# Conditioning weights as the stationary operand in the first modulation of a hybrid diffusion block

## The chip, the core and the metric

One core of a Trainium2 chip runs one program. The metric is the device time of one execution in microseconds (us), and less is better.

## The reference, cut to what matters

The block takes 512 latent tokens and 256 context tokens of width 1024, a conditioning vector `c` and a learned vector `c_ctx`. Everything starts with a modulation: the first 2048 columns of `w_mod` give a shift and a scale for each of the 1024 features, once for the latents and once for the context.

```python
silu_c = jax.nn.silu(c)
silu_cc = jax.nn.silu(c_ctx)
sh_a, sc_a, g_a, sh_f, sc_f, g_f = [m[:, None, :] for m in jnp.split(silu_c @ w_mod[l] + b_mod[l], 6, axis=-1)]
mod_c = jnp.split(silu_cc @ w_mod[l][:, :n_mod * D_MODEL] + b_mod[l][:n_mod * D_MODEL], n_mod, axis=-1)
hc = ctx * (1.0 + mod_c[1]) + mod_c[0]
hx = x * (1.0 + sc_a) + sh_a
```

`hx` and `hc` then go through one input projection `w_in` (z, q, the scan inputs, dt, keys, values), a state-space scan, attention, an output projection and a mixture of experts. All is float32.

## The kernel before, in words

The kernel holds activations turned: `xT` and then `hxh`/`hxl` are [feature in partition, 8 k-tiles, 768 tokens], tokens 0 to 255 context and 256 to 767 latents. Most products are made of three passes over a split of each operand into a high and a low float32r part (`mm3`, L111); the modulation uses plain float32 (`mm`, L108).

`sil` (L215) is [128, 8 k-tiles, 32]: columns 0 and 1 of each k-tile are silu of `c` and `c_ctx`, the other thirty are zero (L216).

The modulation is done in four quarters, h = 0 to 3. `quarter_spec` (L180) says what a piece of weights is: for k-tile kt and quarter h, 256 columns of shift and 256 of scale, [128, 2, 256], 256 KB. A `Stream` (L30) loads pieces over SP's DMA queue (L53) into twelve buffers "mraw" (L198 to L200) and gives them out in order with `take`. A quarter serves the two feature tiles 2h and 2h + 1.

`mod_quarter` (L242) makes one quarter. For each k-tile, a group of four multiplications has 32 columns of `sil` as the stationary operand and 128 columns of weights moving; the four write the four strips of 32 partitions of one PSUM tile "m" (one buffer), [128, 128], in which rows 0 and 1 of a strip are the two conditions. After eight k-tiles VectorE copies "m" to `msb` (L250), PE turns it through the identity into another PSUM tile (L252), and VectorE adds the bias twice (L256) and 1 to the scales (L258), into `modT`: [feature, condition, 16], shift and scale by feature.

`hx_tile` (L261) applies them to one feature tile: two tensor-scalar operations on VectorE (L263), the high part on ScalarE (L265), the low part on VectorE (L266). `x_turn` (L233) turns the token tiles `xin` into `xT`: for each feature tile six PE transposes through PSUM tiles "b" or "t" and copies on ScalarE (L239) and VectorE (L240).

`kv_pass` (L285) is the first user of hx: for each k-tile 6 token tiles x 3 passes = 18 multiplications, 288 moving columns (dt and keys).

Order of work: input loads, `x_turn` of tiles 0 and 1, quarter 0, `x_turn` of 2 and 3, hx tiles 0 and 1, `kv_pass` of k-tiles 0 and 1; then quarters 1, 2, 3 with their hx tiles, the rest of `x_turn` after quarter 1 and `kv_pass` of k-tile 2; k-tile 3 is queued behind the last group of quarter 3 (L309). A planner of the framework turns this program into one queue per engine. It goes by priority (program order, changed by `rank`, L117) and by its own idea of when operands are there; quarters 1 to 3 have a rank ahead of `kv_pass` (L301). So groups of the modulation, turns and key/value multiplications stand mixed in PE's queue, which runs in that order. SP's queue also runs in order: a load whose buffer isn't free holds back the loads behind it, the second half of the input (`x_load(256, 768)`, L273) among them.

The other modulation vectors (gates and the second shift and scale) come later from `mod_rest` (L690) with another function; it uses a PSUM tile "m" and buffers "wraw" of its own.

Of the kernel before, what the change touches and what calls it, by code (L numbers as in the profile page):

```python
# [8 lines left out]
F32 = mybir.dt.float32  # L9
# [86 lines left out]
def hybrid_block_kernel(ctx: ExitStack, tc: tile.TileContext, I, out):  # L96
    nc = tc.nc
    PE, V, S, G, SP = nc.tensor, nc.vector, nc.scalar, nc.gpsimd, nc.sync

    def pool(name, bufs=1, side="left", space=None, stack=None):  # L100
        kw = dict(name=name, bufs=bufs, reuse_waits="tile")
        if space is not None:
            kw["space"] = space
        else:
            kw["side"] = side
        return (stack or ctx).enter_context(tc.tile_pool(**kw))

    def mm(o, a, b, first, last):  # L108
        return PE.matmul(o, lhsT=a, rhs=b, start=first, stop=last)  # L109
# [34 lines left out]
    psa = [pool("psa", 3, space=PSUM, stack=psa_st)]  # L144
# [4 lines left out]
    def pb(tag="b", dt=F32):  # L149
        return psb.tile([128, 512], dt, name=tag, bufs=tags.get(tag, 1))  # L150
# [8 lines left out]
    ident, tri_le, tri_ge = cst[:, 0:128], cst[:, 128:256], cst[:, 256:384]  # L159
# [8 lines left out]
    xtp = pool("xtp", stack=xst)  # L168
# [46 lines left out]
    sil = const.tile([128, 8, 32], F32, name="sil")  # L215
# [25 lines left out]

    def mod_quarter(h):  # L242

        ps = psa[0].tile([128, 512], F32, name="m", bufs=1)[:, 0:128]
        for kt in range(8):
            w = mod0[h].take()
            for i in range(4):
                last = mm(ps[32 * i:32 * i + 32, :], sil[:, kt, :], w[:, i // 2, i % 2 * 128:i % 2 * 128 + 128], kt == 0, kt == 7)
        msb = xtp.tile([128, 128], F32, name="msb", bufs=2)
        V.tensor_copy(msb, ps)  # L250
        p = pb("s" if h == 0 else "t")[:, 0:128]
        PE.transpose(p, msb, ident)  # L252
        pv = p.rearrange("p (s f z) -> p z s f", s=2, f=2)
        part = lambda a: a.rearrange("p (s f) -> p s f", s=2)[:, :, 2 * h:2 * h + 2]
        for r in range(2):
            V.tensor_add(part(modT[:, r, :]), pv[:, r], part(cols[:, C_BM:C_BM + 16]))  # L256
        o = slice(8 + 2 * h, 10 + 2 * h)
        V.tensor_scalar_add(modT[:, :, o], modT[:, :, o], 1.0)  # L258
        return last
# [7 lines left out]

    x_turn(range(2))
    mod_quarter(0)
    win.deep = win.ahead = 0  # L270
    win.fill(0)
# [22 lines left out]
    def six():  # L294
        return dict(zip(order, [pa() for _ in range(3)] + [pb(), pb(), pb("s")]))

    kv_start = tc.cur_priority
    ps = six()
    kv_pass(ps, range(2), 288, 2)
    for h in (1, 2, 3):  # L300
        with rank(kv_start - 3000 + 1000 * h):  # L301
            last = mod_quarter(h)
            if h == 1:
                x_turn(range(4, 8))
        for kt in (2 * h, 2 * h + 1):
            hx_tile(kt)
        if h == 1:
            kv_pass(ps, range(2, 3), 288, 2)
# [54 lines left out]
    ps = six()  # L363
# [440 lines left out]
    def part(g, t, y):  # L804

        p = pa() if g else pb("t")
        for k in range(4):
            PE.transpose(p[:, k * 128:(k + 1) * 128], y[:, k * 128:(k + 1) * 128], ident)
        m = parts[g, t] = (mix, mix2)[g].tile([128, 2, 4, 128], F32R, name=("wraw", "a")[g], bufs=4)
        pv = p.rearrange("p (k q) -> p k q", k=4)  # L810
        S.activation(m[:, 0], pv, AF.Copy)
        V.tensor_sub(m[:, 1], pv, f32(m[:, 0]))
# [843 lines left out]
```

## Time and profile before

| what | us |
|---|---|
| median of 3 runs | 896.88 |
| lowest and highest of them | 889.95, 919.74 |
| the profiled execution | 891.73 |
| its span from the first to the last instruction | 889.9 |

Times in the rows are from the start of the span. Engines: PE is TensorE's multiplications, PEld its loads of the stationary operand, DVE is VectorE, ACT ScalarE, POOL GpSimd, SPq the SyncE queue that issues DMAs. A float32 multiplication leaves two records of MATMUL and two of LDWEIGHTS. The duration of a record includes its way through the engine, so records that follow each other overlap: n like records in T with one lasting d follow at (T - d) / (n - 1). PEclk is the clock granted to TensorE as a share of 2.4 GHz.

### The profile page before, as it was taken

The page shows a single profiled execution, that of the slowest core. Times are in us where ns is not written, and L with a number is a line of the kernel's source. Part 1 is how long each engine was busy: PE and PEld are TensorE (multiplying, and loading weights), DVE is VectorE, ACT ScalarE, POOL GpSimd, SP SyncE. Part 2 cuts the span into 40 slices and gives each one's busy share as a digit, 9 for nine tenths or more (in the row PEclk, how much of TensorE's full clock was granted, in tenths as well). Part 3 has the DMA queues.
Part 4 walks back from the last instruction along what each step waited for, and adds up shares of the span by engine and source line. Part 5 has one row for each costly group of instructions (what it writes and reads, how often), then busy time and mean ns, then how long its engine had stood idle before and what let it go on. Part 6 is the DMA issues. An engine that isn't in the chain of part 4 may idle for free.

```text
span 889.9 us, 14409 instructions
## 1 busy us (share of the span) xinstructions
PE 798.8 (90%) x5328; PEld 604.5 (68%) x5328; DVE 630.3 (71%) x1042; ACT 455.0 (51%) x870; POOL 268.0 (30%) x202
## 2 busy tenths in 40 slices
PE   6998999898989989899999899999982999999783
PEld 3696676566777568677777777787862777777562
DVE  3576665786857896573646566666987999889677
ACT  2253442656743353364544645656461766777452
POOL 0012212313321052510159344600011355544421
PEclk8999999999999999999999999999995999999997
DMA  9966987446522144566052111300459999999964
GB/s 308 321 193 230 299 292 251 124 125 199 144 73 80 30 130 131 194 197 207 18 194 73 36 35 42 119 13 1 143 195 324 343 342 341 338 325 344 341 181 167
DMA packets 112369, 165.59 MB, mean 186 GB/s; under 512 B 13032, under 2 KB 78088, under 8 KB 112296
## 3 DMA queue, kind: packets, MB, share of 16 engines
q1 hardware_dynamic: 105720, 141.76, 49.2%
q0 software_dynamic: 6288, 21.84, 8.6%
q8 instruction: 42, 0.69, 0.3%
q10 hardware_dynamic: 288, 1.05, 0.3%
q14 instruction: 31, 0.25, 0.1%
HBM read 142.41 MB, written 22.21 MB: 185 GB/s over the span
## 4 chain that ended last, share of the span: by engine, by line
PE 59%; DMA 14%; DVE 11%; ACT 6%; issue 5%; POOL 3%; SPq 1%; DVEq 0%; POOLq 0%; ACTq 0%
PE a L109 24%; PE s L109 13%; PE t L109 7%; PE b L963 3%; DMA wraw<-in_w_mod_dram 3%; PE v L109 3%; PE b L109 3%; DMA bc<-csd 2%; PE m L109 2%; DVE acc L475 2%; ACT hxh L957 1%; PE b L1368 1%; DMA wraw<-in_w_up_dram 1%; DMA ml<-in_w_down_dram 1%; DMA ml<-in_w_up_dram 1%
## 5 line engine op out<-in xcount | busy, mean ns | idle before, releaser
L76 ACT ACTIVATE whi<-wraw 128x1024 fp32r<-128x1024 f32 (+1 forms) x100 | 104.2, 1045 | 62.7 <-PE a L109 31.9
L78 DVE TENSOR_TENSOR wlo<-wraw,whi 128x1024 fp32r<-128x1024 f32 (+1 forms) x75 | 95.7, 1282 | 29.3 <-ACT whi L76 29.3
L78 POOL TENSOR_TENSOR wlo<-wraw,whi 128x1024 fp32r<-128x1024 f32 (+1 forms) x20 | 49.3, 2464 | 150.6 <-ACT whi L76 132.2
L956 DVE TENSOR_REDUCE mx<-s 128x1 f32<-128x768 f32 x64 | 61.1, 955 | 29.6 <-PE s L109 24.4
L957 ACT ACTIVATE hxh<-s,mx 128x768 f32<-128x768 f32 x64 | 57.5, 898 | 41.1 <-DVE mx L956 39.5
L475 DVE SCALAR_TENSOR_TENSOR acc<-u,cols,acc 128x770 f32<-128x770 f32 (+1 forms) x48 | 55.4, 1153 | 30.3 <-ACT acc L467 24.3
L109 PE MATMUL a<-whi,hxh 128*128 128x512 f32 (+2 forms) x176 | 69.1, 394 | 1.5 <-ACT hxh L265 1.5
L109 PE MATMUL a<-wlo,hxh 128*128 128x512 f32 (+2 forms) x176 | 69.1, 393 | 0.2 <-DVE wlo L78 0.2
L109 PE MATMUL a<-whi,hxl 128*128 128x512 f32 (+2 forms) x176 | 67.9, 387 | 0.0
L109 PE MATMUL a<-hxh,whi 128*128 128x512 f32 (+1 forms) x176 | 62.5, 355 | 0.0
L109 PE MATMUL a<-hxl,whi 128*128 128x512 f32 (+1 forms) x176 | 62.2, 354 | 0.0
L109 PE MATMUL a<-hxh,wlo 128*128 128x512 f32 (+1 forms) x176 | 61.7, 350 | 0.0
L963 PE MATMUL b<-cst,hxh 128*128 128x128 f32 x384 | 58.7, 277 | 1.7 <-DVE hxh L967 0.5
L592 ACT ACTIVATE bc<-bc,lb 128x128 f32<-128x128 f32 x128 | 40.5, 390 | 23.6 <-POOL bc L589 20.4
L963 PEld LDWEIGHTS b<-cst,hxh 128*128 128x128 f32 x384 | 43.5, 141 | 11.4 <-ACT hxl L937 4.0
L967 DVE COPY hxh<-b 128x512 f32<-128x512 f32 x48 | 33.0, 687 | 16.9 <-PE b L963 16.7
L109 PE MATMUL a<-whi,xh 128*128 128x512 f32 x102 | 44.4, 436 | 0.0
L589 POOL TENSOR_SCALAR_AFFINE_SELECT bc<-bc 128x512 f32<-128x512 f32 x32 | 26.5, 835 | 52.4 <-DMA bc<-csd 50.4
L109 PE MATMUL a<-whi,xl 128*128 128x512 f32 x102 | 41.3, 405 | 0.0
L109 PE MATMUL a<-wlo,xh 128*128 128x512 f32 x102 | 41.2, 404 | 0.0
L1417 POOL DMA_INDIRECT acc<-y,rowi x15 | 28.2, 1881 | 40.8 <-DVE wlo L78 19.4
L109 PEld LDWEIGHTS a<-wlo,hxh 128*128 128x128 f32 x176 | 33.8, 192 | 9.9 <-issue 5.3
(467 smaller groups left out, 2123.2 us busy)
## 6 DMA issues: line engine op xcount, KB each, us to landing
wraw<-in_w_mod_dram SPq DMA_DIRECT2D x32, 512.0 KB
wraw<-in_w_in_dram SPq DMA_DIRECT2D x30, 512.0 KB
wraw<-in_w_down_dram SPq DMA_DIRECT2D x22, 512.0 KB
wraw<-in_w_gate_dram SPq DMA_DIRECT2D x40, 256.0 KB
wraw<-in_w_up_dram SPq DMA_DIRECT2D x40, 256.0 KB
mraw<-in_w_mod_dram SPq DMA_DIRECT2D x32, 256.0 KB
bc<-csd SPq DMA_DIRECT2D x32, 256.0 KB
wraw<-in_w_out_dram SPq DMA_DIRECT2D x15, 512.0 KB
```

Of the source, the lines that this page charges most:

```text
L76: self.nc.scalar.activation(hi, raw, AF.Copy)
L78: self.lo_engine(i).tensor_sub(lo, raw, hi.bitcast(F32))
L109: return PE.matmul(o, lhsT=a, rhs=b, start=first, stop=last)
L475: V.scalar_tensor_tensor(a, uk, wk_, a, op0=OP.mult, op1=OP.add)
L589: G.affine_select(bc[:, d], bc[:, d], pattern=[[0, 4], [sg, 128]], compare_op=OP.is_ge, fill=-1e30, base=0, channel_multiplier=-sg)
L592: S.activation(bc[:, d, h, :], bc[:, d, h, :], AF.Exp, bias=lb[:, c, h0 + h:h0 + h + 1])
L956: V.tensor_reduce(m, x, axis=AX, op=OP.max, negate=True)
L957: S.activation(P[:, g * 768:g * 768 + 768], x, AF.Exp, bias=m, accum_out=sm[u][:, g:g + 1])
L963: PE.transpose(p[:, i * 128:(i + 1) * 128], P[:, (4 * j + i) * 128:(4 * j + i + 1) * 128], ident)
L967: V.tensor_copy(PT[:, o], p)
L1368: PE.transpose(p[:, j * 128:(j + 1) * 128], x[:, k * 128:(k + 1) * 128], ident)
L1417: G.indirect_dma_start(out=acc, out_offset=bass.IndirectOffsetOnAxis(ap=rows, axis=0), in_=y, in_offset=None, compute_op=OP.add)
```

## The change

The weights become the stationary operand, 128 columns at a time, and the two condition columns of `sil` move. The output of a multiplication is [128 features, 2 conditions]; the four of a k-tile write four pairs of columns of an eight-column PSUM tile "m". A multiplication by eight zero columns of `sil` opens the accumulation of all eight columns before k-tile 0. The copy to `msb` and the turn are gone, and the adds of the bias read "m" itself.

```diff
 def mod_quarter(h):
-    ps = psa[0].tile([128, 512], F32, name="m", bufs=1)[:, 0:128]
+    p8 = psa[0].tile([128, 512], F32, name="m", bufs=1)[:, 0:8]
+    p = p8.rearrange("p (s f z) -> p s f z", s=2, f=2)
     for kt in range(8):
         w = mod0[h].take()
-        for i in range(4):
-            last = mm(ps[32 * i:32 * i + 32, :], sil[:, kt, :], w[:, i // 2, i % 2 * 128:i % 2 * 128 + 128], kt == 0, kt == 7)
-    msb = xtp.tile([128, 128], F32, name="msb", bufs=2)
-    V.tensor_copy(msb, ps)
-    p = pb("s" if h == 0 else "t")[:, 0:128]
-    PE.transpose(p, msb, ident)
-    pv = p.rearrange("p (s f z) -> p z s f", s=2, f=2)
+        if kt == 0:
+            mm(p8, w[:, 0, 0:128], sil[:, kt, 2:10], True, False)
+        for s in range(2):
+            for f in range(2):
+                last = mm(p[:, s, f], w[:, s, f * 128:f * 128 + 128], sil[:, kt, 0:2], False, kt + s + f == 9)
+    pv = p.rearrange("p s f z -> p z s f")
     part = lambda a: a.rearrange("p (s f) -> p s f", s=2)[:, :, 2 * h:2 * h + 2]
     for r in range(2):
         V.tensor_add(part(modT[:, r, :]), pv[:, r], part(cols[:, C_BM:C_BM + 16]))
```

## Rows read from the trace of the kernel before

**Rows 1.** The page: busy time by engine, and the clock in forty slices.

```profile
PE 798.8 (90%) x5328; PEld 604.5 (68%) x5328; DVE 630.3 (71%) x1042; ACT 455.0 (51%) x870; POOL 268.0 (30%) x202
...
PEclk8999999999999999999999999999995999999997
```

**Rows 2.** Chain of waits, first 90 us: start, us, what.

```profile
7.72 5.91 DMA mraw<-in_w_mod_dram
13.67 0.47 PE m L109 x8
...
18.18 0.61 PE a L109
```

**Rows 3.** Chain of waits, 60 to 330 us.

```profile
63.49 1.08 PE a L109 x9
...
76.45 1.86 PE m L109 x16
78.93 9.71 DMA wraw<-in_w_mod_dram
```

**Rows 4.** Timeline of SP's queue at 77 us: start, us, what.

```profile
77.47 12.63 SPq L53 DMA_DIRECT2D wraw<-in_w_mod_dram  x7
```

**Rows 5.** Timeline of PE at 48.8 us, in the key/value pass.

```profile
48.85 0.30 PE L109 MATMUL s<-whi,hxl 128*128 128x288 f32 x1
```

**Rows 6.** Timeline at 14 us, VectorE behind quarter 0.

```profile
14.17 0.29 DVE L250 COPY msb<-m 128x128 f32<-128x128 f32 x1 [4.21 <-PE m L109]
...
14.88 0.23 DVE L256 TENSOR_TENSOR modT<-s,cols 128x4 f32<-128x4 f32 x2 [0.42 <-PE s L252]
```

**Rows 7.** Timeline, 9 to 46 us: groups of the modulation on PE.

```profile
9.16 2.68 PE L109 MATMUL m<-mraw,sil 128*32 128x128 f32 x40
...
20.56 0.65 PE L109 MATMUL m<-mraw,sil 128*32 128x128 f32 x8
...
45.37 1.08 PE L109 MATMUL m<-mraw,sil 128*32 128x128 f32 x32
```

**Rows 8.** Groups of weight loads by shape (busy us, mean ns); then a timeline row.

```profile
L109 PEld LDWEIGHTS m<-mraw,sil 128*32 128x32 f32 x256 | 6.4, 120 | 7.8 <-DMA mraw<-in_w_mod_dram 4.1 <-issue 2.2 <-PE s L252 0.7
...
L109 PEld LDWEIGHTS s<-dta,cst 128*128 128x128 f32 x4 | 0.7, 190 | 0.1
...
502.72 0.30 PEld L109 LDWEIGHTS t<-xo,ones 128*128 128x128 f32 x2
```

**Rows 9.** Timeline, 5 to 32 us: weight loads of turns and key/value multiplications.

```profile
5.81 0.18 PEld L238 LDWEIGHTS b<-cst,xin 128*128 128x128 f32 x1 [0.88 <-DVE cols L214]
...
19.71 0.33 PEld L109 LDWEIGHTS a<-wlo,hxh 128*128 128x128 f32 x1
...
19.95 0.33 PEld L109 LDWEIGHTS a<-whi,hxh 128*128 128x128 f32 x1
...
26.07 0.19 PEld L109 LDWEIGHTS a<-whi,hxh 128*128 128x128 f32 x1
...
27.56 0.14 PEld L238 LDWEIGHTS b<-cst,xin 128*128 128x128 f32 x1
...
31.14 0.25 PEld L238 LDWEIGHTS b<-cst,xin 128*128 128x128 f32 x2
```

**Rows 10.** Stretches 14 to 26 us: length, busy us by engine, PEclk, DMA share, GB/s.

```profile
14.00:15.00 1.00, 0.43 (x5) 0.14 (x1) 0.41 (x3) 0.52 (x1) 0.00 (x0) 0.86 1.10 349
...
20.00:22.00 2.00, 2.00 (x14) 1.34 (x14) 0.00 (x0) 0.00 (x0) 0.00 (x0) 0.50 1.00 384
...
24.00:26.00 2.00, 2.00 (x22) 1.01 (x21) 0.00 (x0) 0.00 (x0) 0.00 (x0) 0.76 1.03 383
```

**Rows 11.** Two stretches at the router; a timeline row of its PE work.

```profile
663.30:666.70 3.40, 2.25 (x41) 1.72 (x39) 3.40 (x5) 3.40 (x6) 0.00 (x0) 0.99 1.07 399
666.70:670.10 3.40, 0.17 (x1) 0.10 (x1) 2.32 (x17) 2.18 (x3) 1.14 (x2) 0.50 1.02 397
...
664.46 0.65 PE L109 MATMUL t<-wrA,xo 128*64 128x20 f32 x16
```

## Prediction

> **What bounds the kernel now.** I began with the page's busy shares and its clock line: TensorE (PE) is busy 90% of the span, and the granted clock is at its full level (2.4 GHz) in nearly all of the forty slices [rows 1]. So work taken off or put on PE counts wherever PE is the last to arrive, and a loss of the clock counts twice. Next I read the chain of waits around the change. Until 13.63 us it runs through the landings of the modulation weights; then come the last group of quarter 0 at 13.67 and, over VectorE and ScalarE, the first key/value multiplication at 18.18 [rows 2]. From there to about 77 the chain is PE nearly without a break; the wait of 9.71 at 78.93 is for weights whose loads SP issues from 77.47 on, after the groups at 76.45 have freed their buffers [rows 3, 4]. So nothing behind this stage waits for a fixed time: what the stage loses moves everything behind it, that transfer too. My end of the stage is the last multiplication of key/value k-tile 3, at 48.85 with 0.13 for its pace, or 49.0 [rows 5].
>
> **What is removed.** Four copies of 0.29 and four turns with one 128x128 transpose each. On the path of quarter 0 that is 14.17 to 14.88, or 0.71, in whose place stands one wait for the last multiplication, some 0.3: a gain of 0.4 [rows 6]. For quarters 1 to 3 it lies beside key/value work. I book 0.4 and let it go in the rounding.
>
> **What the multiplications cost before.** An FP32 multiplication leaves two records, so a k-tile's group of four is eight. Forty records at the start took 2.68, eight at the lower clock 0.65, and thirty-two in a row at full clock 1.08 [rows 7]; with the tail of the last taken off that is some 0.25 per group, because the four column strips of 32 run side by side.
>
> **What they cost after.** Each of the four now loads 128x128 weights twice and moves two columns. That is 32 such multiplications per quarter and one for the zeroes, 33, with two records each: 264 records in four quarters. What counts is the load, since two columns can't hide the next one. The loads in the trace grow with their columns: 0.120 for 32, 0.190 for 128, and two 128-column FP32 loads with a short moving part behind each take 0.30 together, so they follow at 0.11 [rows 8]. At the lower clock a 128-column load takes 0.33 and not 0.19, and loads of the key/value pass follow at 0.24 [rows 9]. I take twice 0.11, or 0.22; the bounds are 0.19 (0.11 in the ratio 0.33 to 0.19) and the 0.24 of that pass. So a group costs 0.88 at full clock and 1.76 at half, where it cost 0.25 to 0.65, and the landing of a piece every 0.74 (5.91 for eight [rows 2]) no longer sets the pace.
>
> **At which clock.** This is the term that decides. The page gives 1.00 for the first microseconds, but a turn's load takes 0.18 at 5.81, more than the 0.14 by which the later ones go, so I read the start as the lower level (1.2 GHz) [rows 9]. The granted clock falls at 14.7, after short groups with pauses, and stays at 0.50 until 25 although PE is busy 2.00 of 2.00 from 20 to 22 [rows 10]. It falls again at 666.7, after a stretch in which PE turned tiles and then did two bursts of sixteen router records (the second at 665.71), each with a load; PE had 2.25 of 3.40 busy there and PEld 1.72 [rows 11]. That is the nearest work to the new groups, and it didn't hold the clock. Quarter 0 becomes 14.5 us of such loads. So I take half speed for quarter 0 and for the stretch in which groups of 1.76 stand between four or so key/value multiplications.
>
> **The sum**, with the order of PE's queue left as it is and every gate on PE alone. From 9.16: 264 records at 0.22 are 58.1 (quarter 0 ends at 23.7 and not at 14.1); 72 key/value multiplications of k-tiles 0 to 3 at 0.24 are 17.3; 36 turns of the input at 0.22 (0.11 at full clock: two loads in 0.25 where one takes 0.14 [rows 9]) are 7.9. After each of some 20 groups the next key/value load is no longer hidden by a long multiplication: 20 x 0.2 = 4.0. From this I take 4.4: about twenty turns stand in a row and 18 multiplications follow the last group, 8.7 at half clock, and there the clock may come back. The way over VectorE and ScalarE from 14.88 to 18.18, 3.3 [rows 2, 6], is covered by the two groups of quarter 1 that stand before the first key/value multiplication.
>
> A new wait: the accumulator "m" has one buffer and is now held until both adds of the bias are done (0.23 each [rows 6]) and not only until the copy. Behind it on PE stand the next quarter's zeroing multiplication and all that follows. After quarter 0 PE would wait for the first hx tile anyway; later key/value work may stand between, or not: 0 to 2.4, I take 0.6. SP: the loads of quarter 1's last four pieces wait for buffers that quarter 0 frees until about 16.6, and the input loads behind them come 1 to 2 us later; quarter 0 keeps PE until 23.7, which hides them. POOL gets nothing new.
>
> 9.2 + 58.1 + 17.3 + 7.9 + 4.0 - 4.4 + 0.6 = 92.7, against 49.0: 43.7 later. On the profiled execution's 891.7 (span 889.9 and 1.8 around it) that is **935**. This execution lies 5 below the median of the three times, 896.9, whose spread reaches 919.7; I keep to it. With 0.19 to 0.24 per record and 0 to 8.7 given back, the forecast's own range is 923 to 945.
>
> **Rivals.** *The clock holds* (not slower by what can be told). Quarter 0 is one unbroken stream, so the clock rises in it about as early as it did before and stays: ten records or 2.2 at the lower level, then 254 x 0.11 + 72 x 0.12 (nine in 1.08 [rows 3]) + 36 x 0.11 + 20 x 0.1 + 0.6 and 0.8 of waiting for the first hx tile: 46.1 from 9.2 is 55.3, 6.3 late: 898. It decides as soon as loads follow at 0.11 in quarter 0. For it: PE never pauses, and before, ten microseconds were lost at half clock that would then be won. Against it: 20 to 22 at 0.50 [rows 10], and 666.7 [rows 11]. The Trainium skill's page "TensorE: Matmul & The Clock Gate", section "Why this matters for your kernels", has the rule that speaks for this rival: keep TensorE continuously busy and it comes to the full rate. By that rule the time would be 898, by the rows above 935; the trace agrees with it in the long key/value pass and not from 20 to 22.
>
> *The clock comes back half way*, with the twenty turns: 9.2 + 132 x 0.22 + 24 x 0.24 + 6 x 0.2 + 0.6, then 132 x 0.11 + 48 x 0.12 + 36 x 0.11 + 14 x 0.1, is 71.4: 22.4 late, 914. For it: it rose at 25 out of such a mixture [rows 10]. Against it: groups three times as long stand in the mixture now.
>
> *The moving columns set the price*: two columns in place of 128, loads hidden. Then landing still paces the groups; the last 1.08 of quarter 3 goes from the path [rows 7], and the time is about 890. Against it: the loads at 0.11 apart [rows 8]. By the same page, section "Back-to-back issue gap", an isolated matmul of up to 64 columns takes about 60 cycles, 25 ns as an estimate; 264 of these would be 6.6 us, which is this rival; no run here shows it for FP32 with 128 stationary columns.
>
> **How the numbers follow.** Forecast 0.58, half way 0.15, the clock holds 0.20, moving columns 0.07. About 2% (18 us) is what can be told from no change. Slower by more: the forecast and nearly all of half way, 0.72; within: 0.27; faster: 0.01. The range goes from 898 to 948 (945 and a few for scatter); it leaves out the last rival, half of the one at 898, and 0.03 above.
>
> **What would show it.** After: PEclk low from the start until about 85; loads of "m" as 128x128, 264 of them, 0.33 long and 0.22 apart; quarter 0 ending at 23.7; the first hx multiplication at 27 to 28; the first wait for the later modulation weights near 122 and not 78.9. Loads 0.19 long and 0.11 apart at a granted 1.00 would mean the 898 rival; a first hx multiplication before 18.2 would mean the last. The forecast is wrong, too, if PE's queue is put in another order, with the groups bunched and the key/value multiplications dense between them.

## The result and the profile after

The changed kernel takes 938.93 us in the median of five runs (931.19 to 941.15), the kernel before 896.88: a ratio of 1.0485, 95% interval 1.044 to 1.0531, so it is slower. (The ratio is taken over undisturbed executions only, which leaves out the 919.74 of before.) The profiled execution took 931.19 with a span of 929.4; against the profiled execution of before (891.73, 889.9) that is 39.5 more.

The page of the changed kernel: span, busy line, clock in forty slices, and the group of the new loads (busy us, mean ns, idle before).

```profile
span 929.4 us, 14412 instructions
...
PE 846.3 (91%) x5332; PEld 662.4 (71%) x5332; DVE 633.2 (68%) x1038; ACT 454.4 (49%) x870; POOL 272.1 (29%) x202
...
PEclk9999999999999999999999999999997799999997
...
L109 PEld LDWEIGHTS m<-sil,mraw 128*128 128x128 f32 x264 | 58.8, 333 | 0.8 <-PE m L109 0.4
```

PE is busy 47.5 us longer than in [rows 1] with four more records. 264 loads of 128 columns take 333 ns each, the long form of [rows 9] and not the 190 ns of [rows 8]. And yet the clock line begins with 9s: the page contradicts itself, and the loads decide (last section). The idle time before them is 0.8 in all: 0.4 of it behind the accumulator, as the row says, and 0.4 for weights from memory (the 0.41 at 8.40 in the timeline below), where the old groups had 4.1 of that kind [rows 8].

The chain of waits of the changed kernel, from its start to 140 us (start, us, what).

```profile
8.40 14.25 PE m L109 x66
23.01 2.26 PE m L109 x10
25.72 1.50 PE m L109 x8
...
51.24 0.95 PE t L238 x4
...
60.60 0.96 PE t L238 x4
...
73.88 13.87 PE m L109 x66
...
118.63 1.92 PE m L109 x16
121.04 10.03 DMA wraw<-in_w_mod_dram
```

Where [rows 2] had a chain of landings with short groups behind them, there is now one block of 66 records. The planner put all of quarter 3 into another block of 66. Of the 36 turns behind quarter 0 the rows shown have two fours between groups; the timeline below shows that twenty others stand in a row, from 42.84 to 49. The wait for the later modulation weights, at 78.93 in [rows 3], begins at 121.04: 42.1 later. It was late by what the stage was late.

The timeline of the changed kernel: weight loads (PEld), VectorE's adds of the bias behind quarter 0, the first of the twenty turns in a row, two of the last of them and the group behind, and the last multiplication of k-tile 3.

```profile
8.40 14.15 PEld L109 LDWEIGHTS m<-sil,mraw 128*128 128x128 f32 x66 [0.41 <-DMA mraw<-in_w_mod_dram]
...
22.68 0.23 DVE L256 TENSOR_TENSOR modT<-m,cols 128x4 f32<-128x4 f32 x2 [13.55 <-PE m L109]
...
25.13 0.59 PE L109 MATMUL a<-whi,hxh 128*128 128x288 f32 x1
...
25.28 1.85 PEld L109 LDWEIGHTS m<-sil,mraw 128*128 128x128 f32 x8
...
27.01 0.33 PEld L109 LDWEIGHTS a<-wlo,hxh 128*128 128x128 f32 x1
...
27.23 0.33 PEld L109 LDWEIGHTS a<-whi,hxh 128*128 128x128 f32 x1
...
42.84 0.45 PE L238 MATMUL t<-cst,xin 128*128 128x128 f32 x1
...
47.55 0.63 PE L238 MATMUL b<-cst,xin 128*128 128x128 f32 x2
...
49.54 1.70 PE L109 MATMUL m<-sil,mraw 128*128 128x8 f32 x8
...
91.54 0.29 PE L109 MATMUL s<-whi,hxl 128*128 128x288 f32 x1
```

66 loads in 14.15 with one lasting 0.33 follow at (14.15 - 0.33) / 65 = 0.213. The last row answers to [rows 5]: the stage ends at 91.54 + 0.13 = 91.67 where it ended at 49.0. That is +42.7. From there to 194 us the lag stays about 42 (the first record of L633 starts at 194.2 before and at 236.3 after). Behind that it moves both ways: 38.8 at the last record of L475 (280.9 and 319.7), 39.5 at the first of L956 (408.6 and 448.1), 42.5 at its last (646.4 and 688.9), and 39.5 at the end. The medians of the runs are 42.0 apart. So one pair of executions doesn't show that any of the loss was won back; where the 3 come and go was not followed up.

### The profile page after: what moved, and what is told of

It reads as the page before. It is cut to its first block, busy times and chain, and to the rows that moved or that the text cites. A ratio compares the mean times of both kernels' runs of the same rounds, so it can differ in the third digit from the quotient of the medians.

```text
span 929.4 us, 14412 instructions
## 1 busy us (share of the span) xinstructions
PE 846.3 (91%) x5332; PEld 662.4 (71%) x5332; DVE 633.2 (68%) x1038; ACT 454.4 (49%) x870; POOL 272.1 (29%) x202
## 4 chain that ended last, share of the span: by engine, by line
PE 59%; DMA 14%; DVE 12%; ACT 5%; issue 4%; POOL 3%; SPq 1%; DVEq 0%; POOLq 0%; ACTq 0%
PE a L109 21%; PE s L109 12%; PE m L109 7%; PE t L109 7%; PE b L963 3%; PE b L109 3%; DMA wraw<-in_w_mod_dram 3%; DMA wraw<-in_w_up_dram 3%; DVE acc L475 3%; PE v L109 3%; DMA wraw<-in_w_gate_dram 2%; DMA bc<-csd 2%; DVE wlo L78 2%; ACT hxh L957 1%; PE b L1368 1%
## 5 line engine op out<-in xcount | busy, mean ns | idle before, releaser
L78 DVE TENSOR_TENSOR wlo<-wraw,whi 128x1024 fp32r<-128x1024 f32 (+1 forms) x75 | 98.7, 1322 | 28.7 <-ACT whi L76 28.3
L956 DVE TENSOR_REDUCE mx<-s 128x1 f32<-128x768 f32 x64 | 61.1, 955 | 31.6 <-PE s L109 27.2
L475 DVE SCALAR_TENSOR_TENSOR acc<-u,cols,acc 128x770 f32<-128x770 f32 (+1 forms) x48 | 55.6, 1158 | 29.1 <-ACT acc L467 28.2
L109 PEld LDWEIGHTS m<-sil,mraw 128*128 128x128 f32 x264 | 58.8, 333 | 0.8 <-PE m L109 0.4
L109 PE MATMUL m<-sil,mraw 128*128 128x2 f32 (+1 forms) x264 | 56.5, 343 | 0.4 <-PE m L109 0.4
L109 PE MATMUL a<-whi,xh 128*128 128x512 f32 x102 | 43.7, 429 | 0.0
L589 POOL TENSOR_SCALAR_AFFINE_SELECT bc<-bc 128x512 f32<-128x512 f32 x32 | 28.5, 899 | 51.2 <-DMA bc<-csd 49.1
```

Source lines behind the costliest of these rows:

```text
L78: self.lo_engine(i).tensor_sub(lo, raw, hi.bitcast(F32))
L475: V.scalar_tensor_tensor(a, uk, wk_, a, op0=OP.mult, op1=OP.add)
L589: G.affine_select(bc[:, d], bc[:, d], pattern=[[0, 4], [sg, 128]], compare_op=OP.is_ge, fill=-1e30, base=0, channel_multiplier=-sg)
L956: V.tensor_reduce(m, x, axis=AX, op=OP.max, negate=True)
```

## The experiments

Runs 1 to 4 shared their runs of the kernel before (median 891.34 of 17), runs 5 to 7 theirs (891.64 of 23), runs 8 and 9 theirs (891.32 of 23). These medians lie some 5 below the 896.88 above, so what a run costs is read against its own. "Stage end" is always the last multiplication of k-tile 3 plus 0.13; it was 49.0 before and 91.67 after.

**1. The same loads, 128 moving columns.** From the changed kernel; `wide` holds silu in its first two columns and zeros behind them.

```diff
+wide, zer = ... [128, 8, 128], ... [128, 512]; V.memset(zer, 0.0); V.memset(wide, 0.0); V.tensor_copy(wide[:, :, 0:2], sil[:, :, 0:2])
...
-mm(p8, w[:, 0, 0:128], sil[:, kt, 2:10], True, False)
+mm(p8, w[:, 0, 0:128], zer, True, False)
...
-last = mm(p[:, s, f], w[:, s, f * 128:f * 128 + 128], sil[:, kt, 0:2], False, kt + s + f == 9)
+last = mm(p[:, s, f], w[:, s, f * 128:f * 128 + 128], wide[:, kt, :], False, kt + s + f == 9)
```

> The changed kernel, with the same 128x128 loads, but each load is followed by 128 moving columns (two condition columns and 126 columns of zeroes) and not by two; the zeroing multiplication has 512 columns. Theory (loads set the pace, and the clock stays at half because hardly anything moves): the moving columns now raise the clock early, records of m follow at 0.11 from about 12 us on, and the whole comes to 898 to 902, 30 to 40 below the changed kernel, although TensorE moves 64 times as much in this part. Rival (a load of this kind takes 0.21 at whatever clock, or the clock stays low for another reason): records still follow at 0.21 and the time is that of the changed kernel or above, 932 to 942.

Measured: 902.74 (895.76 to 907.88), ratio 1.0116 [1.0068, 1.0163]. Timeline of this run, weight loads and the last multiplication of the stage:

```profile
10.76 8.02 PEld L109 LDWEIGHTS m<-wide,mraw 128*128 128x128 f32 x63 [0.52 <-issue]
...
20.28 7.11 PEld L109 LDWEIGHTS m<-wide,mraw 128*128 128x128 f32 x63 [0.24 <-issue]
...
57.54 0.29 PE L109 MATMUL s<-whi,hxl 128*128 128x288 f32 x1
```

The second block follows at (7.11 - 0.19) / 62 = 0.112, half of 0.213, and the stage ends at 57.67: +8.7. More work on the moving side, and the kernel is 34 faster at the stage end than the change. So with the loads as they are, the lower clock costs some 34.0 of the 42.7, and the loads at full clock 8.7. The first block still begins at the lower level, (8.02 - 0.19) / 62 = 0.126 on the mean, and the planner moved all of quarter 1 ahead of the first key/value multiplication here, so the 8.7 is that of another order and not quite all at full clock.

**2. The copies and turns alone.** From the kernel before.

```diff
-msb = xtp.tile([128, 128], F32, name="msb", bufs=2)
-V.tensor_copy(msb, ps)
-p = pb("s" if h == 0 else "t")[:, 0:128]
-PE.transpose(p, msb, ident)
+p = ps
```

> The kernel before without its four copies and four turns: the adds of the bias read the accumulator as it is. Left out: the turn of shift and scale, so that modT holds other numbers. Theory (what the change takes away is worth next to nothing): 0.3 to 0.7 less than before, 891 to 897, no difference that can be told. Rival (the wait on the turns was worth something that the change gave back elsewhere): 5 or more below before.

Measured: 896.87 (893.53 to 899.34), ratio 1.0058 [1.0033, 1.0082]: a miss, 5.5 slower with less to do. The stage itself ended 1.5 earlier (47.38 against 48.85). The loss is behind it. Timeline of this run, PE:

```profile
47.38 0.30 PE L109 MATMUL s<-whi,hxl 128*128 128x288 f32 x1
...
62.04 0.58 PE L109 MATMUL b<-whi,hxh 128*128 128x256 f32 x1 [3.39 <-ACT K L361]
```

And VectorE's timeline of the same run:

```profile
56.46 0.19 DVE L360 TENSOR_TENSOR dtr<-b,dtb 128x32 f32<-128x32 f32 x1 [0.20 <-PE b L109]
58.72 2.35 DVE L344 TENSOR_TENSOR tb<-tb,gb 128x256 f32<-128x256 f32 x1 [2.07 <-DMA tb<-in_rope_dram]
...
61.40 0.18 DVE L360 TENSOR_TENSOR dtr<-b,dtb 128x32 f32<-128x32 f32 x1
```

VectorE's timeline of the kernel before has the same preparation:

```profile
58.13 0.41 DVE L344 TENSOR_TENSOR tb<-tb,gb 128x256 f32<-128x256 f32 x1
```

Of the six additions at L360 that help to free the accumulators of the key/value pass, the planner had put two behind the preparation of the rotary tables (L344). In the kernel before even three stand behind it, but VectorE comes to it at 58.13, when its load is there. In run 2 VectorE is there at 56.65, waits 2.07 for the load, and the preparation lasts 2.35 and not 0.41. PE then stands for 3.39, and its clock falls with the pause: granted 0.50 from 62.0 to 64.8, where its thirteen multiplications follow at 0.21 and not at 0.12, some 1.2 more. These 4.6 turn 1.5 ahead into 3 behind; another 2 come behind the wait for the later modulation weights (the first record of L475 is at 101.8, before at 96.7). Run 7 tests this reading.

**3 and 4. The new way in quarter 0 alone, and in quarters 1 to 3 alone.** From the changed kernel:

```diff
+if h == 0:        # run 3; in run 4: if h > 0:
     p8 = psa[0].tile([128, 512], F32, name="m", bufs=1)[:, 0:8]
...
+else:
+    ps = psa[0].tile([128, 512], F32, name="m", bufs=1)[:, 0:128]
...
+    PE.transpose(p, msb, ident)
```

> Quarter 0 by the new way, quarters 1 to 3 by the old one. Theory: quarter 0 ends near 22.6 and not at 14.1, then the old groups follow with less waiting for landings; 4 to 9 above before, 896 to 905. Rival (a loss from the first quarter's chain alone explains the result): 30 or more above before.

Run 3 measured 900.10 (896.28 to 908.08), ratio 1.0094 [1.0062, 1.0126]. Its timeline:

```profile
9.08 14.15 PEld L109 LDWEIGHTS m<-sil,mraw 128*128 128x128 f32 x66 [0.40 <-DMA mraw<-in_w_mod_dram]
```

Quarter 0 costs the same 14.15 as in the changed kernel and ends at 23.2, 9 later than before; 8.8 of that is in the time.

> Quarter 0 by the old way, quarters 1 to 3 by the new one: 198 of the 264 loads. Theory (half clock and 0.213 per load from 15 us on): records of m at 0.21 until the last group, 30 to 37 above before, 922 to 934. Rival (the half clock comes from the long stream of quarter 0 alone; old groups bring the clock up and the mixture then keeps it): records of m at 0.11 from 12 us on for most of the stretch, 5 to 15 above before.

Run 4 measured 929.39 (926.03 to 933.55), ratio 1.0432 [1.0371, 1.0493]. Its stretches (length, busy us of PE, PEld, DVE, ACT and POOL, then PEclk, DMA share, GB/s):

```profile
10.00:12.00 2.00, 1.68 (x28) 0.56 (x24) 0.00 (x0) 0.00 (x0) 0.00 (x0) 1.00 1.05 361
16.00:20.00 4.00, 4.00 (x21) 4.00 (x20) 3.87 (x6) 1.62 (x2) 0.99 (x1) 0.50 1.11 359
20.00:30.00 10.00, 10.00 (x47) 10.00 (x47) 0.34 (x1) 0.00 (x0) 0.00 (x0) 0.50 1.05 375
50.00:70.00 20.00, 20.00 (x93) 19.97 (x93) 7.00 (x13) 4.42 (x7) 0.00 (x0) 0.50 0.34 109
70.00:83.00 13.00, 13.00 (x60) 13.00 (x61) 2.44 (x8) 1.14 (x2) 0.00 (x0) 0.50 0.01 1
83.00:90.00 7.00, 7.00 (x53) 7.00 (x52) 4.81 (x5) 2.94 (x4) 2.33 (x7) 0.97 0.63 164
```

And its timeline, one new group's loads and the end of the stage:

```profile
19.69 1.85 PEld L109 LDWEIGHTS m<-sil,mraw 128*128 128x128 f32 x8
...
84.05 0.29 PE L109 MATMUL s<-whi,hxl 128*128 128x288 f32 x1
```

This is the cleanest proof of the half clock: the page records 0.50 from 15.2 to 83.4, a group has the same 1.85 as in the changed kernel, and from 50 to 83 PE was never idle. In the kernel before the clock rose again at 25 [rows 10]; here, with groups nearly three times as long in the mixture, it came back only after the last of them. Quarters 1 to 3 cost 38.1 of the time, quarter 0 8.8. Their sum, 46.8, is above the 42 to 43 of the whole; the intervals (5.5 to 11.2 and 33 to 44) don't tell these apart.

**5. A version meant to beat both.** From the kernel before: plain multiplications of 256 moving columns beside the old groups of quarters 0 and 1, to have the clock up when key/value work begins.

```diff
 w = mod0[h].take()
+[mm(pb("t")[:, 0:256], ident, w[:, j], True, True) for j in range({0: kt > 3, 1: 2 * (kt < 2)}.get(h, 0))]
```

> The kernel before, with unused multiplications of 256 moving columns into a PSUM tile that nobody reads: one behind each landing of the last four pieces of quarter 0, two behind the first two of quarter 1, where TensorE waits for weights or for the first hx tile. Nothing is left out. Theory (the clock is lost there for want of work, and ten microseconds at half clock cost some 3): the clock rises by 12 and doesn't fall at 14.7, key/value multiplications follow at 0.12 to 0.13 from the first one, and the time is 2 to 4 below before, 887 to 890, the fastest of all. Rival (the stretch is bound by the landings of weights, so a faster clock there buys nothing, or the filler delays the groups): 0 to 3 above before.

Measured: 892.44 (888.12 to 897.32), ratio 1.0026 [0.9997, 1.0056]: no gain. Timeline of PE in this run:

```profile
12.11 1.22 PE L109 MATMUL t<-mraw,cst 128*128 128x256 f32 x2
...
17.08 0.70 PE L109 MATMUL t<-mraw,cst 128*128 128x256 f32 x2
...
22.75 0.40 PE L109 MATMUL a<-whi,hxh 128*128 128x288 f32 x1
```

The clock did rise (1.22 becomes 0.70), but the filler, at half clock itself, put the first key/value multiplication at 22.75 instead of 18.18 [rows 2]. What the clock then gave back was just that: the group that stood at 26.56 before stands at 26.45, and the last multiplication of the stage begins at 49.10, against 48.85 [rows 5]. Runs 8 and 9 try less of it.

**6. Loads of 32 columns in place of 128.** From the changed kernel, with one more multiplication by zeros to end the accumulation.

```diff
-last = mm(p[:, s, f], w[:, s, f * 128:f * 128 + 128], sil[:, kt, 0:2], False, kt + s + f == 9)
+last = mm(p[0:32, s, f], w[:, s, f * 128:f * 128 + 32], sil[:, kt, 0:2], False, False)
...
+last = mm(p8, w[:, 0, 0:128], sil[:, 7, 2:10], False, True)
```

> The changed kernel with loads of 32 columns in place of 128 in all multiplications but the zeroing one and a closing one of the same kind; the queue's order is otherwise the same. Left out: three quarters of the features of shift and scale. Theory (the price of a record is the columns that it loads): records of m follow at 0.05 to 0.08 although the clock stays at half, the groups go back to the pace of the landings, and the time falls by 30 or more against the changed kernel, to 893 to 905. Rival (the price is per instruction, or per switch between load and multiplication): records still follow at about 0.2, 930 to 942.

Measured: 905.55 (898.97 to 912.15), ratio 1.0131 [1.0086, 1.0176]. Its timeline, loads of quarter 0 and the end of the stage:

```profile
10.59 0.50 PEld L109 LDWEIGHTS m<-sil,mraw 128*32 128x32 f32 x8 [0.20 <-DMA mraw<-in_w_mod_dram]
11.31 0.50 PEld L109 LDWEIGHTS m<-sil,mraw 128*32 128x32 f32 x8 [0.22 <-DMA mraw<-in_w_mod_dram]
...
63.02 0.29 PE L109 MATMUL s<-whi,hxl 128*128 128x288 f32 x1
```

The same number of multiplications, with the same two columns moving, follow at (0.50 - 0.16) / 7 = 0.05, a quarter of 0.213, and wait for landings every 0.72 to 0.76 as they did before the change. So the price is that of the columns loaded. The clock stays low: key/value loads last 0.33 until about 62. The stage end, 63.15, is 14.2 late. Half clock by itself costs the key/value multiplications (0.24 and not 0.13) and turns 72 x 0.11 + 36 x 0.11 = 11.9; as an estimate, some 1.5 of it is paid before the change too (fourteen of these multiplications until 25), and the sixteen records with 128 columns that open and close the quarters here add 16 x 0.21 = 3.4. That makes 13.8.

**7. Run 2 again, with the rotary tables behind the key copies.** From run 2.

```diff
-gk, tk = rope_tables(ktp, I["k_norm_g"])
 kv_pass(ps, range(4, 8), 288, 2)
...
     S.activation(K[:, t, :], ps[t][:, 32:288], AF.Copy)
+gk, tk = rope_tables(ktp, I["k_norm_g"])
```

> The run without copies and turns, with the multiplication of the rope tables by the key norm weights placed behind the first key/value adds in the program. Theory (that run gained 1.5 until key/value k-tile 3 and lost 3 and more where VectorE stood before a rope table that hadn't landed, with an add that TensorE waits for behind it): TensorE's wait of 3.4 near 62 is gone and the time is 0 to 2 below before, 888 to 892. Rival (the loss has another cause): it stays at 895 to 898.

Measured: 889.82 (887.29 to 894.58), ratio 0.9991 [0.9966, 1.0015]. VectorE's timeline of this run:

```profile
57.52 0.19 DVE L359 TENSOR_TENSOR dtr<-s,dtb 128x32 f32<-128x32 f32 x1 [0.21 <-PE s L109]
...
59.51 1.93 DVE L344 TENSOR_TENSOR tb<-tb,gb 128x256 f32<-128x256 f32 x1 [1.11 <-DMA tb<-in_rope_dram]
```

All six additions now stand ahead of the tables, PE has no wait between 44 and 78, and the 5.5 are gone. So run 2 lost by the additions that stood behind a preparation whose load was late, as read. The copies and turns are worth 1.2 at the end of the stage (its last multiplication begins at 47.64, not 48.85) and nothing that can be told in the total.

**8 and 9. Filler only in the hole of PE behind quarter 0's turn.** From the kernel before. Run 8:

```diff
 w = mod0[h].take()
+[mm(pb("t")[:, 0:256], ident, w[:, j], True, True) for j in range({1: 2 * (kt == 0) + (kt == 1)}.get(h, 0))]
...
 PE.transpose(p, msb, ident)
+[mm(pb("t")[:, 0:128], ident, msb, True, True) for j in range({0: 3}.get(h, 0))]
```

Run 9 has six of the multiplications behind the turn and none of the others.

> The kernel before with filler multiplications only in the hole of TensorE between the turn of quarter 0 (14.88) and the first key/value multiplication (18.18): three of 128 moving columns behind the turn and three of 256 columns among the first two groups of quarter 1. The earlier filler run brought the clock up but paid for it with a first key/value multiplication at 22.75. Theory: with the filler inside the hole the first key/value multiplication stays near 18.2 to 18.8, the clock is at full level there (multiplications of 288 columns 0.13 apart and not 0.24), and until 25 about twelve of them gain 0.11 each and four groups 0.22 each, some 2.2; the last multiplication of k-tile 3 starts at 46.5 to 47.5 and the time is 1 to 3 below the kernel before (ratio 0.997 to 0.999, at the edge of what five rounds tell). Rival: the stage behind 26 waits for other things (landings of the weights, copies of the turned input), then the last multiplication stays at 48.5 to 49.2 and the time is the same, ratio 1.000. If the clock does not come up, multiplications stay 0.24 apart and the time is 0 to 1 above.

> The kernel before with six filler multiplications of 128 moving columns behind the turn of quarter 0, around the first groups of quarter 1, and nothing else. Less filler than in the run beside it: 12 records of 0.11 to 0.22, or 1.3 to 2.6 of the hole of 3.3. Theory: if that keeps the clock up, the first key/value multiplication stays near 18.2 with the next ones 0.13 apart and the end of k-tile 3 is 1 to 2 earlier than 48.85; if the clock falls all the same, multiplications are 0.24 apart until about 25, the end stays at 48.85 and the time at the kernel before, ratio 1.000. Rival as in the run beside it: the clock is up and the end of the stage stays within 0.3 of 48.85, because something other than TensorE's rate sets it.

Run 8 measured 891.86 (886.69 to 894.9), ratio 1.0012 [0.9979, 1.0044]; run 9 890.9 (887.03 to 897.95), ratio 1.0028 [0.9998, 1.0058]. Neither gains. PE's timeline of run 9:

```profile
15.04 2.34 PE L109 MATMUL t<-msb,cst 128*128 128x128 f32 x6
...
20.52 0.59 PE L109 MATMUL a<-whi,hxh 128*128 128x288 f32 x1
...
23.68 0.29 PE L109 MATMUL a<-wlo,hxh 128*128 128x288 f32 x1
...
49.42 0.29 PE L109 MATMUL s<-whi,hxl 128*128 128x288 f32 x1
```

The filler didn't keep the clock up; it ran at the lower level, and the first six of its twelve records took 2.34. The granted clock came back at 23.1 (0.50 from 22 to 23, 0.96 from 23 to 24), where it was 25 before, but the first key/value multiplication had slipped by 2.3 and the stage ends 0.6 later. In run 8 it slipped to 22.24 and the stage ends 2.2 later. Both expectations of a gain failed, because the filler is paid at the low clock ahead of what it is to speed up. Whether those microseconds of the kernel before can be won in another way stays open; no version here beats it.

## Why the prediction was right, point by point

The forecast was 935, own range 923 to 945; measured 938.93, profiled 931.19. The stage was booked 43.7 late and is 42.7 late. By its steps:

- **The size of the loads.** 264 records were booked at 0.22, 58.1. They follow at 0.213, 56.2. Run 6 shows that the loaded columns set the price; the rival of the moving columns is out.
- **The lower clock.** Right for quarter 0 and for the mixture, by the 0.33 of each load and by run 1. At full clock the loads alone would have cost 8.7 [run 1]; at half clock with cheap loads the stage would have lost 14.2 [run 6]; both together cost 42.7 and not the sum, 22.9, because the lower clock also takes the spacing of 264 loads from 0.112 to 0.213, some 27 (run 6 has records and waits of its own, so the three don't add up exactly).
- **The clock coming back: wrong.** I took 4.4 back for some twenty turns in a row and the 18 multiplications behind the last group. Both came as booked, twenty turns from 42.84 to 49 (with three waits among them, 1.2 in all) and 18 multiplications behind the last block, and the clock didn't: two of the last turns take 0.63 with one lasting 0.42, so they follow at 0.21 as at half clock, and the group behind them takes the same 1.70. Behind the last block the clock rises only at the last four multiplications of k-tile 3, near 91: spacing goes from 0.24 to 0.13 there, some 0.4. Almost nothing was given back. The 8.7 in the lower end of the range was wrong in itself: that is all that these turns and multiplications take at half clock, and full clock gives back half of it, the 4.4 booked. The lower end should have been 927.
- **Exposed key/value loads: wrong by about as much.** I booked 20 x 0.2 = 4.0. The start at 8.40 with 56.2 for the new loads, 72 x 0.24 = 17.3 and 36 x 0.213 = 7.7 makes 89.6; of the 2.1 left to 91.67, the waits of PE take 1.6 (next point). That leaves 0.5. The rows at 25.28 and 27.01 show why: a group's eight loads start while the key/value multiplication ahead still runs, so eight loads and the exposed one behind them fit into 1.73, eight times 0.213 and a rest of 0.03. The two errors cancel, so that the sum fits to 1.0 is partly luck: it had too much by 0.8 (the start), 1.9 (the loads), 3.5 (exposed loads) and 0.4 (turns and "m"), and too little by 4.4 (the clock) and 1.2 (waits in the twenty turns).
- **The new wait on "m"**: booked 0.6, is 0.4, in one place. The other 1.2 are waits of the turns, which the sum had left out. Waits of PE between 8 and 92 us in the changed kernel (total, times, longest):

```profile
PE b L238 <- ACT xT L239: 0.5, 1, 0.5
PE m L109 <- PE m L109: 0.4, 1, 0.4
PE t L238 <- DVE xT L240: 0.4, 1, 0.4
PE t L238 <- ACT xT L239: 0.3, 1, 0.3
```

- **The order.** The first hx multiplication came at 25.13 and not at 27 to 28: the planner put it behind one group of quarter 1 rather than two. Quarter 0 ended at 22.65 (forecast 23.7), 0.8 of it because it began at 8.40 and not at 9.16; in run 3, with the same loads, it began at 9.08, so that start is no part of the change. I had named another order as what would break the forecast. It did change, with quarter 3 in one block, and cost nothing that can be seen: the sum by counts of records still fits to 0.5.
- **Where the loss ends up.** The wait for the later modulation weights was forecast near 122 and came at 121.04: nothing that the stage's end moved was waiting for a fixed time. At the end of the profiled pair 39.5 are left, but the lag was 42.5 at 646 us, and the medians are 42.0 apart.
- **The copies and turns**: booked as a gain of 0.4; run 7 measures 1.2 at the stage. Either is lost beside 43.
- **The rivals of the clock.** Run 1 is the rival "the clock holds" made real, and its sum was near: the stage 6.3 late by forecast, 8.7 measured, and the time 11.4 above its own runs of before. (It took 0.12 for a key/value multiplication from nine with 256 moving columns; those of the stage have 288 and follow at 0.13, which makes it 0.7 more.) "Half way" is out: the twenty turns came in a row and the clock stayed down. The rule of the Trainium skill that spoke for the first (the page "TensorE: Matmul & The Clock Gate", section "Why this matters for your kernels": keep TensorE continuously busy and it reaches the full rate) did not hold for this work: in run 4 PE was busy 20.00 of 20.00 us from 50 to 70 at a granted 0.50. The measurement decides.

## What to carry to other kernels

A product with few rows on one side should be priced by the columns that it loads as stationary, one load per FP32 record: here eight records of a group took 1.70 (8 x 0.213) where four strips side by side took 0.25 to 0.65 [rows 7], and that outweighs any copy or turn saved. Before an edit that turns a stream into loads with next to nothing moving, price it at both clock levels, and ask what else shares the queue, since the lower clock is paid by that too (14.2 here with cheap loads). When removing small work makes a kernel slower, look at what the engines now come to too early, in their order, before doubting the price.

## What the runs showed of the hardware that was not expected

- **The page's clock can read full when the engine isn't.** Stretches of the changed kernel (columns as in run 4):

```profile
10.00:12.00 2.00, 2.00 (x11) 2.00 (x11) 0.00 (x0) 0.00 (x0) 0.00 (x0) 1.00 1.08 367
35.00:40.00 5.00, 5.00 (x24) 5.00 (x25) 0.00 (x0) 0.00 (x0) 0.00 (x0) 1.00 0.24 74
85.00:90.00 5.00, 5.00 (x23) 5.00 (x24) 2.15 (x8) 0.84 (x2) 0.00 (x0) 1.00 0.00 0
```

  PEclk is 1.00 in all of them, with the same 0.33 loads that run 4 has at a recorded 0.50. My reading is that the page shows the full level until the first change of the clock is recorded, which in this run is near 91 (run 6 shows the same, 1.00 from 8 to 66 with 0.33 loads until 62); the prediction had used the same reading for the first microseconds of before, and its forecast of a low PEclk until about 85 failed on this. The duration of a 128-column FP32 load (0.33 or 0.19) told the level every time.
- **Pauses aren't needed for the lower level.** In the kernel before, the clock fell behind short groups with pauses [rows 10, 11]. In run 4 it stayed at 1.2 GHz from 50 to 83 us without one. Behind the same loads, 128 moving columns instead of two brought 0.112 by the second block. What in the moving part does it was not tried further.
- **A rise of the clock can cost what it brings**: run 5 had it at 17 instead of 25, run 9 at 23.1, and neither ended the stage earlier, because the work that came before the rise held the queue at half speed.
